# x transposed and weights laid out by chunk on the host, x loaded through buffers of its own

## The chip, the cores and the metric

The kernel runs on one core of a Trainium2 chip. Its time is the device time of one execution in microseconds. A core has five engines with an instruction queue each: PE (TensorE, matrix products), DVE (VectorE), ACT (ScalarE), POOL (GpSimd) and SP (SyncE, which here only issues DMAs), and sixteen DMA engines that they share. Each engine takes its instructions in order.

## What is computed

One layer of a decoder: x is 512 tokens by 2048. One projection gives queries, keys, values and gates for 16 heads of three kinds and six forget gates (`ff`), then attention per head, a gate, an output projection and a layer norm:

```python
h = x @ w_in                                  # 512x2048 @ 2048x8198
(fq, fk, fv, fg, sq, sk, sv, sg, dq, dk, dv, dg, ff) = jnp.split(h, _split_points(), axis=-1)
log_f = jax.nn.log_sigmoid(ff + b_f)
o_fox = forgetting_attention(fq, fk, fv, log_f) * jax.nn.silu(fg)     # 6 heads
o_sb  = stick_breaking_attention(sq, sk, sv) * jax.nn.silu(sg)        # 6 heads
o_d   = differential_attention(dq, dk, dv, lam, slopes)               # 4 heads, rms-normed
o_d   = o_d * subln_g * (1.0 - lam_init) * jax.nn.silu(dg)
y = jnp.concatenate([o_fox, o_sb, o_d], axis=-1) @ w_out
return layernorm(alpha * x + y, ln_g, ln_b)
```

## The kernel before

Every product is made in three passes of a faster, shorter number format (fp32r): an operand is split into a high part (a cast, `h` at the end of its name, on ACT) and a low part (operand minus high part, `l`, on DVE), and `mm3` (line 112) makes high by high, high by low and low by high. So each loaded tile costs a cast and a subtraction before PE can use it (`split`, line 124).

PE contracts over the 128 partitions, so x must lie with its 2048 columns on the partitions: 16 k-tiles of 128 columns by 512 tokens, x0 to x15. x comes as 512 x 2048 from memory. `load_x` (line 303) loads 256 columns at a time, with rows of 1 KB, and `transpose_x` (line 311) turns each k-tile with four PE transposes into a PSUM bank `xt`, from which ACT and DVE take the two parts. For the 12 k-tiles of chunk groups 1 to 3 (`SJ`) ACT also keeps a copy `xc`, from which `x_sums` (line 322) makes four sums on GpSimd (`s`) that are split too (`xs`): they serve a seven-product scheme for the later units (`seven`, line 196).

The first stage multiplies the columns of units 0 and 1 (512 columns) in eight chunks "f" of two k-tiles each (loop at line 725), into four PSUM banks p0a to p0d. Later units u = 2 to 31 have 256 columns and four chunks of four k-tiles ("u", line 161); the attention of the heads runs between them at unit times given by `at_unit`, and `tick` counts those times. At the end come the output projection ("o" chunks) and the layer norm.

Weights are loaded two chunks ahead (`load_chunk`, line 158, on SP) into the tag `raw`, which has three buffers (line 149). The loads of x take buffers of the same tag. A chunk "f" is two DMAs with rows of 1 KB, a chunk "u" one DMA with rows of 1 KB, a chunk "o" one with rows of 2 KB. PE's order is written by hand (`pin`); the order on the other engines is set by a scheduler when the kernel is built.

The start (lines 678 to 699): SP issues the first half of x's first tile, then the weights of the first k-tile, then the other half, then the second k-tile's weights. PE runs five warm-up products, the first transposes, three more warm-ups, and the first product.

Of the kernel before, what the change touches and what calls it, by code (L numbers as in the profile page):

```python
# [70 lines left out]
SEVEN = (1, 5, 7, 6, 2, 4, 3)  # L71
BANK = {1: ("a", 0), 6: ("a", 1), 5: ("b", 0), 7: ("b", 1), 2: ("c", 0), 4: ("c", 1), 3: ("d", 0)}
H2 = S // 2
SECOND = [60] * 7 + [55]


@with_exitstack
def trunk(ctx, tc, x, w_in, b_f, lam_p, subln_g, w_out, ln_g, ln_b, out):
    nc = tc.nc
    V, A, G, T = nc.vector, nc.scalar, nc.gpsimd, nc.tensor  # L80

    xf = x[0]
    w1 = w_in[0].rearrange("(kt p) c -> p kt c", p=P)
    w2 = w_out[0].rearrange("(kt p) c -> p kt c", p=P)
    of = out[0]

    const = ctx.enter_context(tc.tile_pool(name="const", bufs=1))
# [46 lines left out]
    A.preload_act_table_set("natural_log_exp_and_others")  # L134

# [14 lines left out]

        return tuple(wpool.tile(shape, F32R, tag=f"{tag}{s}", bufs=2, name=f"w{s}{name}") for s in "hl")

    def first_cols(k0, k1):
        return [(i * 256, w1[:, k0:k1, c:c + 256]) for i, c in enumerate(head_cols(PAIRS[0][0])[:2])]

    def load_chunk(n):

        kind, g, j = chunks[n]  # L160
        if kind == "u":
            raw = raw_tile(f"raw{n}", [P, 4, 256])
            c0 = head_cols(PAIRS[g // 4][0])[g % 4]
            nc.sync.dma_start(raw, w1[:, 4 * j:4 * j + 4, c0:c0 + 256])
            if j in SJ:
                ready[n] = seven(n, raw)
            else:
                parts = part_tiles(n, [P, 4, 256])
                split(*parts, raw)
                ready[n] = [tuple(t[:, k] for t in parts) for k in range(4)]  # L170
            return
        raw = raw_tile(f"raw{n}", [P, KC, 512])
        if kind == "f":
            for dst, src in first_cols(j * KC, (j + 1) * KC):
                nc.sync.dma_start(raw[:, :, dst:dst + 256], src)
        else:
            k0, c0 = ORDER[j * KC], g * 512
            nc.sync.dma_start(raw, w2[:, k0:k0 + KC, c0:c0 + 512])
        if n >= RES or n % 3 == 2:
            ready[n] = []  # L180
            for k in range(KC):
                if n < RES:
                    hi, lo = part_tiles(f"{n}_{k}", [P, 512], "t2")
                elif slots_left:
                    hi, lo = kx_pair(slots_left.pop(0), [P, 512], f"w{n}_{k}")
                else:
                    hi, lo = [fin.tile([P, 512], F32R, name=f"w{n}_{k}{s}") for s in "hl"]
                ready[n].append((hi, lo))
                pin(A.copy(hi, raw[:, k]))  # L189
                pin(V.tensor_tensor(out=lo, in0=raw[:, k], in1=hi.bitcast(F32), op=ALU.subtract))  # L190
        else:
            parts = part_tiles(n, [P, KC, 512])
            split(*parts, raw)
            ready[n] = [tuple(t[:, k] for t in parts) for k in range(KC)]
# [20 lines left out]
    def load_late(dst, src):  # L215

        pin(nc.sync.dma_start(dst, src))
# [68 lines left out]
    with ExitStack() as actx:  # L286
# [6 lines left out]
            return at.tile([P, 1], F32, tag="st", bufs=24, name=name)  # L293


        xv = xf.rearrange("(tb p) c -> p tb c", p=P)
# [4 lines left out]
        copies = {}  # L301

        def load_x(c):
            xraw[c] = raw_tile(f"xr{c}", [P, NT, 256])
            if c > 0:
                x_part(c, 0, 256)

        def x_part(c, c0, c1):
            nc.sync.dma_start(xraw[c][:, :, c0:c1], xv[:, :, c * 256 + c0:c * 256 + c1])

        def transpose_x(kt):
            c, s = divmod(kt, 2)
            pt = (psL, psL, psT, psO)[kt % 4](f"xt{kt}")
            for tb in range(NT):
                transpose(pt[:, tb * P:(tb + 1) * P], xraw[c][:, tb, s * P:(s + 1) * P], ident)
            for cs, hi, lo in x_parts(kt):
                split(hi, lo, pt[:, cs])
            if kt // 4 in SJ:
                copies[kt] = wk(f"xc{kt}")
                A.copy(copies[kt], pt)  # L320

        def x_sums(j, i):

            ka, kb = copies.pop(4 * j + i), copies.pop(4 * j + 2 + i)
            a11, a21, a12, a22 = ka[:, :H2], ka[:, H2:], kb[:, :H2], kb[:, H2:]
            s = wpool.tile([P, 4, H2], F32, tag="t", bufs=1, name=f"s{j}_{i}")
# [29 lines left out]

        def ff_start():
            wf = at.tile([P, NK, NF], F32, name="wf")
            load_late(wf, w1[:, :, O_FF:O_FF + NF])
            bfc = at.tile([NF, 1], F32, name="bfc")  # L360
            load_late(bfc, b_f.rearrange("a h -> h a"))

# [332 lines left out]
        at_unit(4, lambda: load_x(3))  # L695
        at_unit(7, lambda: load_x(4))
        at_unit(11, lambda: load_x(5))
        at_unit(15, lambda: load_x(6))
        at_unit(19, lambda: load_x(7))
# [15 lines left out]
        acc = [bank(0, b) for b in "abcd"]  # L715

        def product(n, k, c, part=None):
            kt = chunks[n][2] * KC + k
            hi, lo = ready[n][k]
            ps = slice(c * P, (c + 1) * P)  # L720
            for cs, bh, bl in x_parts(kt):
                mm3(acc[c][:, cs], hi[:, ps], lo[:, ps], bh, bl, kt == 0 and cs.start == 0,
                    kt == NK - 1 and cs.stop == S, part)

        for n in range(NJ):
            if n == 0:
                load_chunk(AHEAD)
                for k in range(KC):
                    for part in range(3):
                        for c in range(4):  # L730
                            if k == KC - 1 and part == 2:
                                tick()
                            product(n, k, c, part)
                        if k == 0 and part == 0:
                            transpose_x(1)
                        if k == 1 and part < 2:
                            transpose_x(2 + part)
            for c in range(4) if n > 0 else ():
                if c == 0:
                    load_ahead(n)  # L740
# [204 lines left out]

_INS = ["x", "w_in", "b_f", "diff_lambda", "diff_subln_g", "w_out", "ln_g", "ln_b"]
_OUTS = [((1, S, D), "float32")]


# [20 lines left out]
```

## Time and profile before

| | |
|---|---|
| median of 3 runs | 986.35 us (985.11 to 986.51) |
| the profiled execution | 988.49 us, of which the span shown in the profile is 986.3 |
| PE busy | 962.0 us, 98% of the span |
| DVE busy | 758.6 us, 77% |
| ACT busy | 524.7 us, 53% |
| GpSimd busy | 138.1 us, 14% |
| DMA | 108.76 MB, 110 GB/s in the mean |
| share of the chain that ended last | PE 84%, DVE 6%, DMA 4% |

A row of the order of time reads: start, duration, engine, line, operation, what is written and read, shapes, and in brackets how long the engine had been idle before it and what ended that. Durations of matmuls overlap: the distance from one start to the next is the pace. "PEclk" is the granted clock of PE, where 1.00 is 2.4 GHz and 0.50 is 1.2 GHz. A row of waits reads: who waited for whom, microseconds in total, how often, the longest.

### The profile page before, as it was taken

How to read it: one execution, taken by the hardware profiler on the slowest of the kernel's cores; microseconds unless marked ns; L12 is line 12 of the kernel's file. 1: busy time of each engine (PE TensorE's matmuls, PEld its weight loads, DVE VectorE, ACT ScalarE, POOL GpSimd, SP SyncE). 2: the span in 40 equal slices, each digit the busy share in tenths (PEclk: the TensorE clock that was granted, in tenths of full speed). 3: DMA queues.
4: the chain of work that ended last, by engine and by line, in shares of the span. 5: the costliest groups of instructions: out<-in, count | busy, mean ns of one | idle time of the engine just before them, and what ended most of it. 6: DMA issues, size and time to landing. Idle time of an engine off the chain costs nothing.

```text
span 986.3 us, 16851 instructions
## 1 busy us (share of the span) xinstructions
PE 962.0 (98%) x6466; PEld 882.8 (90%) x6466; DVE 758.6 (77%) x1388; ACT 524.7 (53%) x977; POOL 138.1 (14%) x162
## 2 busy tenths in 40 slices
PE   8998999999999999999999999999999999999994
PEld 7887999999999998999899999999999978888884
DVE  4588888889888988899999887778877863442558
ACT  4665574566466645765675566556745762121222
POOL 0431030113002200120011011010210110000026
PEclk9999999999999999999999999999999999999998
DMA  6443233333332333233323333343333733933313
GB/s 193 150 114 86 67 98 116 86 86 97 97 107 76 108 96 86 73 89 107 98 71 103 106 108 97 99 121 104 105 98 96 224 109 96 348 90 106 98 54 148
DMA packets 92200, 108.76 MB, mean 110 GB/s; under 512 B 6098, under 2 KB 76882, under 8 KB 91864
## 3 DMA queue, kind: packets, MB, share of 16 engines
q1 hardware_dynamic: 88184, 96.15, 33.6%
q10 hardware_dynamic: 3456, 9.96, 2.8%
q0 software_dynamic: 480, 1.57, 0.6%
q8 instruction: 51, 0.84, 0.4%
q14 instruction: 29, 0.24, 0.1%
HBM read 99.80 MB, written 7.88 MB: 109 GB/s over the span
## 4 chain that ended last, share of the span: by engine, by line
PE 84%; DVE 6%; DMA 4%; issue 3%; ACT 2%; SPq 0%; POOL 0%; ACTq 0%; DVEq 0%; POOLq 0%
PE o L107 10%; PE l L107 3%; DMA raw<-in_w_in_dram 3%; PE pt L110 2%; PE po0a L107 1%; PE po0d L107 1%; PE po0c L107 1%; PE po0b L107 1%; PE po2d L107 1%; PE po2c L107 1%; PE po2b L107 1%; PE po2a L107 1%; DVE wl L122 1%; DVE y L906 1%; PE p16c L107 1%
## 5 line engine op out<-in xcount | busy, mean ns | idle before, releaser
L122 DVE TENSOR_TENSOR wlt<-t,wht 128x1024 fp32r<-128x1024 f32 x90 | 110.7, 1230 | 18.0 <-ACT wht L127 17.9
L122 DVE TENSOR_TENSOR wl<-raw,wh 128x1024 fp32r<-128x1024 f32 x53 | 65.3, 1232 | 68.0 <-ACT wh L127 67.6
L127 ACT CAST wht<-t 128x1024 fp32r<-128x1024 f32 x90 | 94.2, 1047 | 28.2 <-DVE t L204 14.7
L127 ACT CAST wh<-raw 128x1024 fp32r<-128x1024 f32 x53 | 55.5, 1048 | 74.9 <-PE po2d L107 27.6
L127 ACT CAST wha<-raw 128x512 fp32r<-128x512 f32 x90 | 55.6, 618 | 48.5 <-PE p18c L107 3.6
L122 DVE TENSOR_TENSOR wla<-raw,wha 128x512 fp32r<-128x512 f32 x90 | 65.7, 730 | 16.8 <-ACT wha L127 16.6
L201 DVE TENSOR_TENSOR t<-raw 128x512 f32<-128x512 f32 x90 | 64.8, 720 | 0.5
L525 ACT ACTIVATE u<-u,m 128x128 f32<-128x128 f32 (+3 forms) x56 | 31.5, 562 | 51.4 <-DVE m L522 51.1
L122 DVE TENSOR_TENSOR wld<-raw,whd 128x256 fp32r<-128x256 f32 x90 | 49.9, 555 | 0.3
L127 ACT CAST pth<-pt 128x128 fp32r<-128x128 f32 (+1 forms) x64 | 26.9, 421 | 23.3 <-PE pt L110 23.2
L204 DVE TENSOR_TENSOR t<-raw,t 128x256 f32<-128x256 f32 x90 | 37.8, 420 | 1.5
L203 DVE TENSOR_TENSOR t<-raw,t 128x256 f32<-128x256 f32 x90 | 38.0, 422 | 0.9
L472 POOL TENSOR_TENSOR g<-g,ge 128x512 f32<-128x512 f32 x16 | 26.9, 1683 | 83.2 <-ACT ge L471 83.2
L127 ACT CAST whd<-raw 128x256 fp32r<-128x256 f32 x90 | 36.0, 400 | 4.5 <-PE p21d L107 1.6
L483 POOL TENSOR_TENSOR mx<-mx,g 128x512 f32<-128x512 f32 x14 | 20.5, 1466 | 119.6 <-issue 101.0
L538 POOL TENSOR_SCALAR_AFFINE_SELECT d<-d 128x128 f32<-128x128 f32 x24 | 14.6, 610 | 160.3 <-ACT d L537 144.8
L122 DVE TENSOR_TENSOR ptl<-pt,pth 128x128 fp32r<-128x128 f32 (+1 forms) x64 | 30.9, 483 | 5.2 <-ACT pth L127 5.0
L901 POOL TENSOR_TENSOR y<-y,gb 128x512 f32<-128x512 f32 (+1 forms) x8 | 12.0, 1521 | 157.8 <-ACT y L900 157.8
L190 DVE TENSOR_TENSOR wl<-raw,wh 128x512 fp32r<-128x512 f32 x22 | 17.0, 792 | 18.7 <-ACT wh L189 18.7
L782 DVE TENSOR_TENSOR e<-e 128x256 f32<-128x256 f32 x30 | 13.7, 456 | 18.9 <-ACT e L781 18.3
L558 POOL TENSOR_SCALAR_AFFINE_SELECT e<-e 128x128 f32<-128x128 f32 x24 | 10.4, 434 | 117.9 <-DVE e L557 98.2
L189 ACT CAST wh<-raw 128x512 fp32r<-128x512 f32 x22 | 13.3, 620 | 25.5 <-PE o L107 11.1
(6721 smaller groups left out, 3849.4 us busy)
## 6 DMA issues: line engine op xcount, KB each, us to landing
raw<-in_w_in_dram SPq DMA_DIRECT2D x120, 512.0 KB, 3.8
raw<-in_w_out_dram SPq DMA_DIRECT2D x32, 512.0 KB, 3.9
xr<-in_x_dram SPq DMA_DIRECT2D x7, 512.0 KB, 3.5
raw<-in_w_in_dram SPq DMA_DIRECT2D x14, 256.0 KB, 4.0
mixd<-mx SPq DMA_DIRECT2D x14, 256.0 KB, 2.0
mr<-mixd ACTq DMA_DIRECT2D x14, 256.0 KB, 4.7
out_dram<-y SPq DMA_DIRECT2D x14, 256.0 KB, 2.4
y<-in_x_dram ACTq DMA_DIRECT2D x4, 768.0 KB, 11.7
```

What stands on the lines that cost most here:

```text
L107: pin(T.matmul(ps, lhs, rhs, start=start, stop=stop))
L110: pin(T.transpose(dst, src, idt))
L122: V.tensor_tensor(out=lo, in0=src, in1=hi.bitcast(F32), op=ALU.subtract)
L127: A.copy(hi, src)
L190: pin(V.tensor_tensor(out=lo, in0=raw[:, k], in1=hi.bitcast(F32), op=ALU.subtract))
L201: V.tensor_tensor(out=t[:, 0:2], in0=raw[:, :, P:].rearrange("p (b k) c -> p b k c", b=2), in1=raw[:, 0:2].rearrange("p k (b c) -> p b k c ...
L203: V.tensor_tensor(out=t[:, 2], in0=b22, in1=t[:, 0], op=ALU.subtract)
L204: V.tensor_tensor(out=t[:, 3], in0=b21, in1=t[:, 2], op=ALU.subtract)
L472: G.tensor_tensor(out=c, in0=c, in1=e, op=ALU.mult)
L483: G.tensor_tensor(out=mx, in0=mx, in1=gt[h], op=ALU.mult)
L525: A.activation(u[:, :n], u[:, :n], AF.Exp, bias=m, scale=-1.0, accum_out=sm)
L538: G.affine_select(out=dt_[:, i * P:n], in_=dt_[:, i * P:n], pattern=[[-1, P]], base=0, channel_multiplier=1, compare_op=ALU.is_ge, fill=BIG)
```

## The change

x is transposed on the host (`x_t`, eight pieces n of two k-tiles, 4 KB for each partition), and the weights are laid out so that each chunk is one run of memory, with 4 KB for each partition. The transposes of x on PE are gone; ACT and DVE split the loaded x itself, and the sums read it too, so the copies `xc` are gone. The pieces of x take the tags `t`, `ptl`, `e` and `pth` (`XTAGS`) in place of `raw`; these tags are used later by the attention and the seven-product scheme. A piece holds k-tiles 4j + i and 4j + i + 2, the pair that a sum needs, and a chunk "f" now multiplies that pair. The first weights are issued by ACT, the first x by SP; the load of ACT's table comes behind them, and the warm-ups stand together: ten.

```diff
+XTAGS = ["t", "ptl", "e", "pth", "ptl", "e", "ptl", "e"]
...
     def load_chunk(n):
...
             raw = raw_tile(f"raw{n}", [P, 4, 256])
-            c0 = head_cols(PAIRS[g // 4][0])[g % 4]
-            nc.sync.dma_start(raw, w1[:, 4 * j:4 * j + 4, c0:c0 + 256])
+            nc.sync.dma_start(raw, w_in[g - 2, j])
...
         if kind == "f":
-            for dst, src in first_cols(j * KC, (j + 1) * KC):
-                nc.sync.dma_start(raw[:, :, dst:dst + 256], src)
+            nc.sync.dma_start(raw, w_first[j])
         else:
-            k0, c0 = ORDER[j * KC], g * 512
-            nc.sync.dma_start(raw, w2[:, k0:k0 + KC, c0:c0 + 512])
+            nc.sync.dma_start(raw, w_out[g, j])
...
-        def load_x(c):
-            xraw[c] = raw_tile(f"xr{c}", [P, NT, 256])
-            if c > 0:
-                x_part(c, 0, 256)
...
-        def transpose_x(kt):
-            c, s = divmod(kt, 2)
-            pt = (psL, psL, psT, psO)[kt % 4](f"xt{kt}")
-            for tb in range(NT):
-                transpose(pt[:, tb * P:(tb + 1) * P], xraw[c][:, tb, s * P:(s + 1) * P], ident)
-            for cs, hi, lo in x_parts(kt):
-                split(hi, lo, pt[:, cs])
-            if kt // 4 in SJ:
-                copies[kt] = wk(f"xc{kt}")
-                A.copy(copies[kt], pt)
-
-        def x_sums(j, i):
-
-            ka, kb = copies.pop(4 * j + i), copies.pop(4 * j + 2 + i)
-            a11, a21, a12, a22 = ka[:, :H2], ka[:, H2:], kb[:, :H2], kb[:, H2:]
+        def load_x(n):
+
+            pool = wpool if XTAGS[n] == "t" else at
+            xraw[n] = pool.tile([P, 2, S], F32, tag=XTAGS[n], bufs=1, name=f"xr{n}")
+            if n > 0:
+                nc.sync.dma_start(xraw[n], xt[n])
+
+        def split_x(n, ks=(0, 1)):
+            j, i = divmod(n, 2)
+            for k in ks:
+                for cs, hi, lo in x_parts(4 * j + 2 * k + i):
+                    split(hi, lo, xraw[n][:, k, cs])
+
+        def x_sums(n):
+
+            j, i = divmod(n, 2)
+            r = xraw.pop(n)
+            a11, a21, a12, a22 = r[:, 0, :H2], r[:, 0, H2:], r[:, 1, :H2], r[:, 1, H2:]
...
         load_x(0)
-        x_part(0, 0, 128)
         first = raw_tile("raw0", [P, KC, 512])
         ready[0] = [part_tiles(f"0_{k}", [P, 512], "t2") for k in range(KC)]
         for k in range(KC):
-            for dst, src in first_cols(k, k + 1):
-                nc.sync.dma_start(first[:, k, dst:dst + 256], src[:, 0])
-            if k == 0:
-                x_part(0, 128, 256)
-                transpose_x(0)
-                warm_up(3)
+            nc.sync.dma_start(xraw[0][:, k], xt[0, :, k])
+            nc.scalar.dma_start(first[:, k], w_first[0, :, k])
+        A.preload_act_table_set("natural_log_exp_and_others")
+        for k in range(KC):
+            split_x(0, (k,))
             hi, lo = ready[0][k]
             V.tensor_copy(hi, first[:, k])
             V.tensor_tensor(out=lo, in0=first[:, k], in1=hi.bitcast(F32), op=ALU.subtract)
+        warm_up(5)
         load_x(1)
         load_chunk(1)
-        at_unit(1, lambda: load_x(2))
...
-        for kt in range(4, NK):
-            at_unit(kt // 2 * 4 - 3 + kt % 2, lambda kt=kt: transpose_x(kt))
-        for n, j in enumerate(SJ):
-            for i in range(2):
-                at_unit(11 + 8 * n + 3 * i, lambda j=j, i=i: x_sums(j, i))
+        load_x(2)
+        split_x(1)
+        for n in range(3, NJ):
+            at_unit(max(1, 4 * n - 11), lambda n=n: load_x(n))
+        for n in range(2, NJ):
+            at_unit(4 * n - 6, lambda n=n: split_x(n))
+        for n in range(NJ):
+            if n // 2 in SJ:
+                at_unit(4 * n + 1, lambda n=n: x_sums(n))
...
         def product(n, k, c, part=None):
-            kt = chunks[n][2] * KC + k
+            kt = n // 2 * 4 + n % 2 + 2 * k
...
-                        if k == 0 and part == 0:
-                            transpose_x(1)
-                        if k == 1 and part < 2:
-                            transpose_x(2 + part)
...
+        x_t=a["x"][0].T.reshape(NK // 4, 2, 2, P, S).transpose(0, 2, 3, 1, 4).reshape(NK // 2, P, 2, S),
+        w_first=_np.concatenate([w1[..., c:c + 256] for c in units[:2]], -1).reshape(
+            NK // 4, 2, 2, P, 512).transpose(0, 2, 3, 1, 4).reshape(NK // 2, P, 2, 512),
+        w_in=_np.stack([w1[..., c:c + 256].transpose(0, 2, 1, 3) for c in units[2:]]),
```

On PE, at the start of the program, the order was (the names: `warm` the warm-ups, `xt` the transposes, `p0a` to `p0d` the four banks of the first stage, `wh` and `wl` the parts of the weights; the number behind a name is that of a buffer):

```order
L107 MATMUL warm<-ones_78 128x128 x5
L110 MATMUL xt_162<-ident,xr_152 128x128 x4
L107 MATMUL warm<-ones_78 128x128 x3
L107 MATMUL p0a<-x0h,wh_0_155 128x512
L107 MATMUL p0b<-x0h,wh_0_155 128x512
L107 MATMUL p0c<-x0h,wh_0_155 128x512
L107 MATMUL p0d<-x0h,wh_0_155 128x512
L110 MATMUL xt_206<-ident,xr_152 128x128 x4
L107 MATMUL p0a<-x0l,wh_0_155 128x512
```

and is now, at the same place:

```order
L106 MATMUL warm<-ones_77 128x128 x10
L106 MATMUL p0a<-x0h,wh_0_153 128x512
L106 MATMUL p0b<-x0h,wh_0_153 128x512
L106 MATMUL p0c<-x0h,wh_0_153 128x512
L106 MATMUL p0d<-x0h,wh_0_153 128x512
L106 MATMUL p0a<-x0l,wh_0_153 128x512
```

The eight warm-ups have become ten in one piece, and products follow on products; no row with `xt` is left on PE, and from the first product of unit 2 on its 5949 rows are those of before.

On SP, from the second load of x in the start on, the order of the DMAs was (`xr` a piece of x, `raw` a chunk of weights):

```order
L309 DMA xr_178<-in_x_dram 128x4x256
L175 DMA raw_180<-in_w_in_dram 128x2x256 x2
L175 DMA raw_191<-in_w_in_dram 128x2x256 x2
L309 DMA xr_244<-in_x_dram 128x4x256
L175 DMA raw_249<-in_w_in_dram 128x2x256 x2
L309 DMA xr_256<-in_x_dram 128x4x256
L309 DMA xr_298<-in_x_dram 128x4x256
L175 DMA raw_306<-in_w_in_dram 128x2x256 x2
```

and is now, from the load of x5 to that of x7 (x5 is `xr_288`, x6 `xr_355`, x7 `xr_418`; `raw_527` and `raw_605` are chunks 8 and 9, the first two of unit 2; `raw_684` is chunk 10):

```order
L298 DMA xr_288<-in_x_t_dram 128x1024
L168 DMA raw_336<-in_w_first_dram 128x1024
L168 DMA raw_403<-in_w_first_dram 128x1024
L168 DMA raw_466<-in_w_first_dram 128x1024
L158 DMA raw_527<-in_w_in_dram 128x1024
L209 DMA wf<-in_w_ff_dram 128x96
L209 DMA bfc<-in_b_f_dram 6x1
L298 DMA xr_355<-in_x_t_dram 128x1024
L158 DMA raw_605<-in_w_in_dram 128x1024
L298 DMA xr_418<-in_x_t_dram 128x1024
L158 DMA raw_684<-in_w_in_dram 128x1024
```

Loads of x and weights took turns before; now the first six pieces of x stand among the first chunks and x6 and x7 stand behind all chunks of the first stage.

## Rows read from the trace of the kernel before

**Rows 1.** Busy time by stage: stretch, length, busy (count) per engine, clock, DMA share, GB/s.
```profile
0.00:64.40 64.40, 60.32 (x344) 52.04 (x345) 37.55 (x68) 36.02 (x72) 17.21 (x27) 0.97 0.59 165
64.40:250.00 185.60, 182.86 (x1342) 171.94 (x1342) 159.98 (x273) 109.53 (x204) 33.13 (x45) 0.99 0.32 90
```

**Rows 2.** Waits of PE, whole run: us in total, times, longest.
```profile
PE pt L110 <- ACT rs L566: 2.7, 1, 2.7
PE l L107 <- DVE vl L122: 2.0, 2, 1.5
PE po0a L107 <- DVE wl L190: 1.2, 1, 1.2
```

**Rows 3.** Chain of waits in the first stage: start, us, what.
```profile
8.57 0.38 SPq L175
...
8.99 3.25 DMA raw<-in_w_in_dram
12.27 1.06 ACT wh L127
...
13.35 1.24 DVE wl L122
14.60 0.37 SPq L175
...
43.38 0.37 SPq L175
```

**Rows 4.** Order of time of PE, start of the run.
```profile
1.12 2.50 PE L107 MATMUL warm<-ones 128*128 128x128 f32 x10 [1.12 <-DVE ones L239]
...
4.59 1.49 PE L107 MATMUL warm<-ones 128*128 128x128 f32 x6
6.00 0.77 PE L107 MATMUL p0a<-x0h,wh 128*128 128x512 f32 x1
...
7.56 0.60 PE L110 MATMUL xt<-ident,xr 128*128 128x128 f32 x4
...
17.72 1.06 PE L110 MATMUL xt<-ident,xr 128*128 128x128 f32 x4
18.43 0.78 PE L107 MATMUL p0b<-x2h,wh 128*128 128x512 f32 x1
```

**Rows 5.** Order of time of PE, later in the first stage.
```profile
21.01 0.60 PE L110 MATMUL xt<-ident,xr 128*128 128x128 f32 x4
21.37 0.48 PE L107 MATMUL p0c<-x2h,wh 128*128 128x512 f32 x1
21.68 0.39 PE L107 MATMUL p0c<-x2l,wh 128*128 128x512 f32 x1
...
57.54 0.28 PE L107 MATMUL p0d<-xa3h,wh 128*128 128x256 f32 x1
...
58.98 0.40 PE L107 MATMUL p0a<-x14h,wh 128*128 128x512 f32 x1
...
64.44 0.28 PE L107 MATMUL p2a<-xa1h,wha 128*128 128x256 f32 x1
```

**Rows 6.** Windows of PE: stretch, length, busy (count), granted clock, DMA share, GB/s.
```profile
18.00:19.00 1.00, 1.00 (x5) 0.50 0.58 156
...
386.00:388.00 2.00, 0.50 (x4) 1.00 0.00 0
...
390.00:392.00 2.00, 2.00 (x11) 0.50 0.64 220
```

**Rows 7.** DMA: GB/s in 40 slices of 0:60, then of 834:860; issues of x, us to landing.
```profile
GB/s 0 193 197 281 282 96 112 285 262 210 222 270 210 178 11 194 374 131 0 134 289 234 41 25 306 129 239 11 1 285 319 94 11 54 307 36 276 60 126 247
...
GB/s 76 236 343 139 28 176 230 199 268 296 290 227 369 432 444 372 372 397 388 369 416 425 425 444 425 444 388 422 457 375 441 419 403 444 400 347 406 378 391 151
...
xr<-in_x_dram SPq DMA_DIRECT2D x7, 512.0 KB, 3.5
```

**Rows 8.** The fourth sum of each set on GpSimd: duration min/median/max in ns.
```profile
L330 POOL TENSOR_TENSOR s<-xc,s x6: 787/858/1072, 32.0 to 73.7; 128x256 f32<-128x256 f32 x6
```

More of the change, by code (lines that the diff above doesn't have):

```diff
@@ L73, with trunk @@
 H2 = S // 2
+XTAGS = ["t", "ptl", "e", "pth", "ptl", "e", "ptl", "e"]
 SECOND = [60] * 7 + [55]
 @with_exitstack
-def trunk(ctx, tc, x, w_in, b_f, lam_p, subln_g, w_out, ln_g, ln_b, out):
+def trunk(ctx, tc, x, xt, w_first, w_in, w_ff, b_f, lam_p, subln_g, w_out, ln_g, ln_b, out):
     nc = tc.nc
@@ L82, in trunk @@
     xf = x[0]
-    w1 = w_in[0].rearrange("(kt p) c -> p kt c", p=P)
-    w2 = w_out[0].rearrange("(kt p) c -> p kt c", p=P)
     of = out[0]
@@ L132, in split @@
                                    op0=ALU.mult, op1=ALU.subtract)
-    A.preload_act_table_set("natural_log_exp_and_others")
     NJ = NK // KC
@@ L153, in part_tiles @@
         return tuple(wpool.tile(shape, F32R, tag=f"{tag}{s}", bufs=2, name=f"w{s}{name}") for s in "hl")
-    def first_cols(k0, k1):
-        return [(i * 256, w1[:, k0:k1, c:c + 256]) for i, c in enumerate(head_cols(PAIRS[0][0])[:2])]
     def load_chunk(n):
@@ L293, in st @@
             return at.tile([P, 1], F32, tag="st", bufs=24, name=name)
-        xv = xf.rearrange("(tb p) c -> p tb c", p=P)
         xraw = {}
@@ L300, in trunk @@
                           for s, (t, b) in zip("hl", ((("g0", 1), ("g1", 1)), (("mx", 2), ("mx", 2)), (("vh0", 1), ("vl0", 1)))[i]))
-        copies = {}
-        def load_x(c):
-            xraw[c] = raw_tile(f"xr{c}", [P, NT, 256])
-            if c > 0:
-                x_part(c, 0, 256)
-        def x_part(c, c0, c1):
-            nc.sync.dma_start(xraw[c][:, :, c0:c1], xv[:, :, c * 256 + c0:c * 256 + c1])
-        def transpose_x(kt):
-            c, s = divmod(kt, 2)
-            pt = (psL, psL, psT, psO)[kt % 4](f"xt{kt}")
-            for tb in range(NT):
-                transpose(pt[:, tb * P:(tb + 1) * P], xraw[c][:, tb, s * P:(s + 1) * P], ident)
-            for cs, hi, lo in x_parts(kt):
-                split(hi, lo, pt[:, cs])
-            if kt // 4 in SJ:
-                copies[kt] = wk(f"xc{kt}")
-                A.copy(copies[kt], pt)
-        def x_sums(j, i):
-            ka, kb = copies.pop(4 * j + i), copies.pop(4 * j + 2 + i)
-            a11, a21, a12, a22 = ka[:, :H2], ka[:, H2:], kb[:, :H2], kb[:, H2:]
-            s = wpool.tile([P, 4, H2], F32, tag="t", bufs=1, name=f"s{j}_{i}")
+        def load_x(n):
[12 more added lines that the diff above has]
+            a11, a21, a12, a22 = r[:, 0, :H2], r[:, 0, H2:], r[:, 1, :H2], r[:, 1, H2:]
+            s = wpool.tile([P, 4, H2], F32, tag="t", bufs=1, name=f"s{n}")
             G.tensor_tensor(out=s[:, 0], in0=a21, in1=a22, op=ALU.add)
@@ L358, in ff_start @@
             wf = at.tile([P, NK, NF], F32, name="wf")
-            load_late(wf, w1[:, :, O_FF:O_FF + NF])
+            load_late(wf, w_ff)
             bfc = at.tile([NF, 1], F32, name="bfc")
@@ L691, in trunk @@
             V.tensor_tensor(out=lo, in0=first[:, k], in1=hi.bitcast(F32), op=ALU.subtract)
+        warm_up(5)
         load_x(1)
         load_chunk(1)
-        at_unit(1, lambda: load_x(2))
[L695 to L699, printed above, removed]
-        for kt in range(4, NK):
-            at_unit(kt // 2 * 4 - 3 + kt % 2, lambda kt=kt: transpose_x(kt))
-        for n, j in enumerate(SJ):
-            for i in range(2):
-                at_unit(11 + 8 * n + 3 * i, lambda j=j, i=i: x_sums(j, i))
+        load_x(2)
[7 more added lines that the diff above has]
+                at_unit(4 * n + 1, lambda n=n: x_sums(n))
         at_unit(40, constants)
@@ L944, in trunk, with _layout @@
         layer_norm(t)
-_INS = ["x", "w_in", "b_f", "diff_lambda", "diff_subln_g", "w_out", "ln_g", "ln_b"]
+_INS = ["x", "x_t", "w_first", "w_in", "w_ff", "b_f", "diff_lambda", "diff_subln_g", "w_out", "ln_g", "ln_b"]
 _OUTS = [((1, S, D), "float32")]
+def _layout(inputs):
+    import numpy as _np
+    a = {k: _np.asarray(v) for k, v in inputs.items()}
+    w1 = a["w_in"][0].reshape(NK // 4, 4, P, -1)
+    units = [head_cols(h)[i] for h, _ in PAIRS for i in range(4)]
+    w2 = a["w_out"][0].reshape(NK, P, D)[ORDER].reshape(NK // KC, KC, P, 4, 512)
+    return dict(
+        a,
+        x_t=a["x"][0].T.reshape(NK // 4, 2, 2, P, S).transpose(0, 2, 3, 1, 4).reshape(NK // 2, P, 2, S),
+        w_first=_np.concatenate([w1[..., c:c + 256] for c in units[:2]], -1).reshape(
+            NK // 4, 2, 2, P, 512).transpose(0, 2, 3, 1, 4).reshape(NK // 2, P, 2, 512),
+        w_in=_np.stack([w1[..., c:c + 256].transpose(0, 2, 1, 3) for c in units[2:]]),
+        w_ff=w1[..., O_FF:O_FF + NF].transpose(2, 0, 1, 3).reshape(P, NK, NF),
+        w_out=w2.transpose(3, 0, 2, 1, 4),
+    )
 def kernel(**inputs):
@@ L959 @@
     nc = _bacc.Bacc("TRN2", target_bir_lowering=False, num_devices=1)
+    inputs = _layout(inputs)
     arrays, args = {}, []
```

## The prediction

> **What bounds the kernel now.** I read the busy time by stage first [rows 1]. PE is busy for 60.32 of the first 64.40 us and for 182.86 of the next 185.60. The first 64.40 us are the stage that the change rewrites: x is loaded, split and multiplied with the first 512 weight columns, in eight chunks of two k-tiles. Its DMA rate is only 165 GB/s and its granted clock 0.97, against 0.99 in the next. Next come PE's waits [rows 2]: three places after the first stage hold 2.7, 2.0 and 1.2 us, the whole run has little more. So PE is the bound nearly everywhere, and time can only be won where PE does work that can go, or where it is slow inside the first stage.
>
> Two things are slow there. The chain of waits [rows 3] shows one closed loop: SP issues a chunk of weights at 8.57, it lands 3.25 us later, ACT takes the high part (1.06), DVE the low part (1.24), and only then, at 14.60, SP issues the next one, since the freed `raw` buffer was what it waited for. x and the weights share three `raw` buffers. From 8.57 to 43.38 the loop turns five times, 6.96 us each. PE's own order of time [rows 4] shows what this does: the first product starts at 6.00, but at 17.72 four transposes that take 0.36 us at 21.01 [rows 5] take 0.71, and the granted clock there is 0.50 [rows 6], that is 1.2 GHz in place of 2.4, after a stretch in which PE had mostly waited for splits.
>
> **Part by part.** The sum is made on the profiled execution: 988.49 us, span 986.3.
>
> *The products themselves* don't change. A 512-wide chunk without transposes goes from 58.98 to 64.44 [rows 5]: 5.46 us for 24 matmuls, 0.2275 each. Twelve 256-wide ones go from 57.54 to 58.98, 0.12 each. Before, five chunks are 512-wide and three are wholly 256-wide: 5 x 5.46 + 3 x 48 x 0.12 = 44.58 us. After, the pairing of k-tiles is another (0 and 2, 1 and 3, and so on), so six chunks are half and half: 2 x 5.46 + 6 x (12 x 0.2275 + 24 x 0.12) = 44.58. Equal.
>
> *The stage before* lasts from 6.00 to 64.44, 58.44 us, so 13.86 us are not products.
>
> *The transposes of x go.* Fifteen groups of four lie inside this stretch. A group and the first product behind it last from 21.01 to 21.68, 0.67 us where a product alone takes 0.2275 [rows 5]: 0.44 each, 15 x 0.44 = 6.6 us. They stand on PE, which has no slack behind them, so this is a plain gain, whether the clock was full or not. The twelve ACT copies that kept x for the sums go too; ACT doesn't set the end, so I cost them at nothing.
>
> *The rest of the 13.86*, 7.26 us, is the slow start of the first four products (6.00 to 7.56, 1.56 us where four take 0.91 [rows 4]: 0.65 us), waits for splits and the half clock. The 0.65 stays, since the same warm-ups stand ahead of it. The other 6.6 us go if the loads come in time.
>
> *Do they?* x now has four tags of its own and `raw` is left to weights, so the loads of chunk 0 to 2 wait for no engine. Before chunk 1 is complete, 2.10 MB must land. In the first microseconds the DMA moved 193, 197, 281 and 282 GB/s in slices of 1.5 us from 1.5 on [rows 7], with runs of 512 B and 1 KB; at their mean, 238, the 2.10 MB are there at 1.5 + 8.8 = 10.3, the high part at 11.4, the low part at 12.6. PE comes to chunk 1 at 6.0 + 0.65 + 5.46 = 12.1 and needs the low part with its third matmul at 12.6. So even the old rate nearly does; where rows of 2 KB and more were moved, the rate was 347 to 457 [rows 7], and by that the data are there at 6 to 8 us. After that one chunk (1.05 MB) needs 4.4 us even at 238 and PE 5.6, so the loads gain on PE. I take 0.4 us of new waits, between 0 and 1.5.
>
> The Trainium skill (DMA: Bandwidth & Descriptors, "Where 436 GB/s comes from") states that for transfers from HBM the HBM side binds at about 358 GB/s for a core. The rows with 444 and 457 lie above it, so here the measurement decides; by 358 chunk 1 would be there at 7.4 and the sum would be the same 973.5.
>
> *The start.* Before, x waited for the transposes and the weights came behind it on SP. After, the ten warm-ups stand in one piece on PE. Each is two records: five took 2.50 us and three took 1.41 from start to start [rows 4], so ten take 4.7 to 5.0 from 1.12 and end at 5.8 to 6.1. The first product needs 512 KB: at 238 GB/s from 1.5 on that is 3.7, and with one cast of x and of w it is ready before 6. So the warm-ups set the start, and it stays at 6.0: the two queues are worth nothing, between -0.3 and +0.3.
>
> The Trainium skill (DMA: Bandwidth & Descriptors, "Rules for kernel authors") speaks against that part as well: DMAs from several issuers run on the same engines, so a second queue saves issue time and brings no bandwidth. The issue time here is 0.43 us for each of the two loads; if it counted, the sum would be 972.6, and by the row on the warm-ups it is 973.5.
>
> *The late x.* `ptl` and `e` each hold several x chunks in turn, so x6 is loaded only when GpSimd has made the four sums of x4, and x7 when it has made those of x5; both stand in SP's queue among the weights of chunks 8 and 9, which wait behind them. A sum takes up to 0.86 us at the median [rows 8], a set 3.4; the next set waits for the splits of the last, which I price like a weight split, 1.06 + 1.24: 5.7 us for a round. x2 lands at 1.5 + 2.62 MB / 238 = 12.5. The sums of x4 end at 12.5 + 2 x 5.7 + 3.4 = 27.3 and x6 lands 3.5 us later [rows 7], 30.8; x7 at 36.5. PE needs them at 40.0 and 45.6. Hidden, with about 7 us to spare after the split.
>
> *What follows the stage.* PE's later rows are the same in the same order, those of ACT, DVE and GpSimd but for a few neighbours. The waits of 2.7, 2.0 and 1.2 us end on splits and weights of units behind this stage [rows 2], made by instructions that stand as before, so I keep them. The weights for later units land sooner, but no wait of PE ends on them: nothing.
>
> Sum: 6.6 + 6.6 - 0.4 = 12.8 us. The profiled execution would be 988.49 - 12.8 = 975.7. It lay 2.14 above the median of the runs, so the median goes from 986.35 to **973.5**.
>
> **Rivals.** (A) *The loop of loads stays the pace.* For it: it fills the chain today. Against: `raw` is now three deep for weights alone. If chunk 7's weights still came at 43.38 + 6.02 (one turn up to the low part), PE would end the stage 5.6 later at 55.0, a gain of 9.4: 977.0. (B) *The DMA rate is the bound.* At the stage's mean of 165 GB/s the 8.39 MB need 50.8 us; with 1.5 ahead and 2.3 + 5.6 behind, the stage ends at 60.2: gain 4.2, 982.1. At 152 GB/s nothing is won. Against: that mean has idle gaps in it, and busy slices were at 281. (C) *Slower: the late x.* A round of sums and splits of r us makes x7 usable at 12.5 + 3r + 3.4 + 3.5 + 2.3; PE stalls from r = 8, and the kernel is slower than before by over 0.2% from r = 13. At r = 14 x7 is 18 us late: 991.6. For it: GpSimd, ACT and DVE run in order, and a split can stand behind a cast that waits for PE. Against: 5.7 from rows. (D) *One new gap and a slow clock.* An idle time of 1.5 us, the longest of the second line [rows 2], lies in the window 386 to 388, and from 390 to 392 the granted clock was 0.50 [rows 6]; the half clock of the first stage lasted from 17.7 to 21.0, which costs half of that, 1.7. Such a gap costs 1.5 + 1.7: 976.7. (E) *The later waits move with the phase:* all three gone, 5.9 less, 967.6, or as much again, 979.4. That the transposes would stay in some form is excluded by PE's order.
>
> **How the numbers follow.** Chances: forecast 0.58 (its own range 972 to 975), A 0.12, B 0.06 (half of it without gain), C 0.04, D 0.08, E 0.06 each way. Beside these the bounds of the new waits are 0 to 1.5. A range from 970 to 979 holds the forecast, A, D and some of E, about 0.8. Faster by over 0.2% (about 2 us, what a measurement here can tell from no change): 0.93; within: 0.03; slower: 0.04.
>
> **What would show it.** Right: no transposes of x; first product near 6.0; PE's first product of unit 2 near 51.5 in place of 64.44; clock 1.00 through that stage; x6 and x7 landing before 40; the wait of 2.7 us still there, some 13 us earlier. Wrong: PE waiting for `wh`, `wl` or x in chunks 1 and 2 (A, B, D), or for x6 and x7 in chunks 6 and 7 (C); a start later than 6.3; PE's time after the stage changed by over 3 us (E).

## The result and the profile after

The changed kernel took 972.84 us at the median of four runs (972.36 to 976.25), the kernel before 986.43 beside it (985.11 to 987.38): a ratio of 0.9871, with a 95% interval of 0.9845 to 0.9896. The forecast was 973.5. The profiled execution of after took 972.67, its span is 970.9; before it was 988.49 and 986.3. So the two profiled executions differ by 15.8 us, the medians by 13.6; the profiled run of before lay 2.1 above its median.

The busy time by stage, in the same columns as [rows 1], with the cut where the first stage now ends:

```profile
0.00:51.40 51.40, 50.27 (x292) 45.11 (x293) 40.62 (x70) 30.75 (x63) 23.22 (x28) 1.00 0.62 206
51.40:237.00 185.60, 182.93 (x1354) 172.05 (x1353) 159.88 (x275) 110.37 (x204) 31.49 (x43) 1.00 0.29 91
```

The first stretch is 13 us shorter than in [rows 1] and PE is busy for all of it but the 1.1 us ahead of the warm-ups; the mean granted clock went from 0.97 to 1.00. The second is as busy as it was (182.93 of 185.60, against 182.86).

PE's order of time at the start and at the end of the stage (start, us, what):

```profile
1.13 4.63 PE L106 MATMUL warm<-ones 128*128 128x128 f32 x20 [1.13 <-DVE ones L231]
5.41 0.68 PE L106 MATMUL p0a<-x0h,wh 128*128 128x512 f32 x1
5.93 0.40 PE L106 MATMUL p0b<-x0h,wh 128*128 128x512 f32 x1
...
50.45 0.28 PE L106 MATMUL p2a<-xa1h,wha 128*128 128x256 f32 x1
```

From the first product to the first of unit 2 it is now 45.04 us, where the products alone are 44.58; in [rows 4, 5] it was 58.44. PE's waits over the whole run (us in total, times, longest):

```profile
PE pt L109 <- ACT rs L551: 2.7, 1, 2.7
PE l L106 <- DVE vl L121: 1.9, 2, 1.5
PE warm L106 <- DVE ones L231: 1.1, 1, 1.1
PE po0a L106 <- DVE wl L182: 0.6, 1, 0.6
```

None lies in the first stage. The three waits of [rows 2] are all still there, some 14 us earlier.

**Where the time went.** Laying PE's rows of both traces side by side and subtracting their starts, the lead of after is 14.0 us at the first product of unit 2 (64.44 against 50.45), and 0.6 of that is the earlier first product. It grows by 1.3 where before ran at 1.2 GHz behind the 2.7 us wait, and by 0.7 in two places behind 780 us (0.6 of it the shorter wait for `po0a`): 15.95 at 928. The tail gives 0.55 back. The 1.3 is the granted clock (last but two in a row) of this stretch of before:

```profile
97.00:98.00 1.00, 1.00 (x7) 1.00 (x6) 1.00 (x3) 0.37 (x1) 0.00 (x0) 0.50 1.02 347
98.00:99.00 1.00, 1.00 (x6) 1.00 (x6) 1.00 (x2) 0.59 (x1) 0.00 (x0) 0.50 0.32 112
```

and of after at the same place of the program:

```profile
83.00:84.00 1.00, 1.00 (x11) 1.00 (x10) 1.00 (x2) 0.90 (x2) 0.00 (x0) 1.00 0.89 365
```

The wait ahead of it was 2.7 us in both kernels, and the clock fell in one of the two executions. It isn't the change that decides this, as the run with one queue shows below.

### The profile page after: what moved, and what is told of

It reads as the page before. It is cut to its first block, busy times and chain, and to the rows that moved or that the text cites. A ratio compares the mean times of both kernels' runs of the same rounds, so it can differ in the third digit from the quotient of the medians.

```text
span 970.9 us, 16701 instructions
## 1 busy us (share of the span) xinstructions
PE 949.8 (98%) x6406; PEld 873.8 (90%) x6406; DVE 759.1 (78%) x1388; ACT 518.7 (53%) x965; POOL 141.9 (15%) x162
## 4 chain that ended last, share of the span: by engine, by line
PE 89%; DVE 5%; issue 3%; DMA 1%; ACT 1%; POOL 0%; ACTq 0%; SPq 0%; DVEq 0%; POOLq 0%
PE o L106 10%; PE l L106 3%; PE pt L109 2%; PE p0a L106 1%; PE p0b L106 1%; PE po0a L106 1%; PE po0b L106 1%; PE po0d L106 1%; PE po0c L106 1%; PE po2d L106 1%; PE po2c L106 1%; PE po2b L106 1%; PE po2a L106 1%; PE p0c L106 1%; PE p0d L106 1%
## 5 line engine op out<-in xcount | busy, mean ns | idle before, releaser
L106 PE MATMUL o<-ptl,vh 128*128 128x256 f32 x96 | 26.9, 280 | 0.0
```

The lines of the kernel that those rows point to most:

```text
L106: pin(T.matmul(ps, lhs, rhs, start=start, stop=stop))
```

## The experiments

### What the transposes of x cost by themselves

The changed kernel, with 15 groups of four PE transposes of a constant put where the transposes of x had stood; nothing reads them.

```diff
+        def idle_transposes(kt):
+            pt = (psL, psL, psT, psO)[kt % 4](f"xt{kt}")
+            for tb in range(NT):
+                transpose(pt[:, tb * P:(tb + 1) * P], ident, ident)
...
+        for kt in range(4, NK):
+            at_unit(kt // 2 * 4 - 3 + kt % 2, lambda kt=kt: idle_transposes(kt))
...
+                        if k == 0 and part == 0:
+                            idle_transposes(1)
+                        if k == 1 and part < 2:
+                            idle_transposes(2 + part)
```

> The changed kernel with 15 groups of four PE transposes (of the identity, read by nobody) put back at the places where those of x stood; loads, buffers and splits stay as changed. Theory (PE is the bound in the first stage, so each group costs 0.44 us there): 15 x 0.44 = 6.6 us slower than the changed kernel, about 979.5 us, the stage ending near 57.0 in place of 50.45, no wait of PE in it. Rival (the transposes lay in time in which PE would have waited for loads, and the loads are the gain): within 1 us of 972.8.

Measured: 979.23 us (978.75 to 982.22), ratio 0.9936 [0.9915, 0.9957], so 6.4 more than after. Its first product starts at 5.20, and the stage ends here:

```profile
56.74 0.28 PE L106 MATMUL p2a<-xa1h,wha 128*128 128x256 f32 x1
```

That is 51.54 us, 6.5 more than after, or 0.43 for a group; the prediction read 0.44 from [rows 5]. No wait came with them. The transposes are a plain cost on the engine that sets the end, and they are half of the gain.

### The other half: own buffers, the layout, and both

Three runs look for the other half. First before's kernel with x in the four tags of its own and nothing else changed:

```diff
-            xraw[c] = raw_tile(f"xr{c}", [P, NT, 256])
+            pool = wpool if XTAGS[c] == "t" else at
+            xraw[c] = pool.tile([P, NT, 256], F32, tag=XTAGS[c], bufs=1, name=f"xr{c}")
```

> The kernel before with one edit: the pieces of x take the tags t, ptl, e and pth in place of raw; transposes, short rows and the order of the first loads stay. Theory: the waits and the half clock of the first stage go, 5 to 6.6 us faster than before, 980 to 981.5 us; the 15 groups of transposes stay. Rival (short rows at 250 to 280 GB/s keep the pace): within 2 us of 986.4.

Measured: 983.53 (981.54 to 984.57), ratio 0.9971 [0.9958, 0.9983]: 3.0 us less than before, so between the two expectations. There is no half clock in its stage (granted 1.00 throughout, in this one execution), yet the stage still takes 54.96 us from 6.01:

```profile
60.97 0.28 PE L108 MATMUL p2a<-xa1h,wha 128*128 128x256 f32 x1
```

Second, before's kernel with only the weights laid out by chunk:

```diff
-            for dst, src in first_cols(j * KC, (j + 1) * KC):
-                nc.sync.dma_start(raw[:, :, dst:dst + 256], src)
+            nc.sync.dma_start(raw, w_first[j])
```

> The kernel before with one edit: all weights laid out by chunk, so that each chunk is one run of memory with 4 KB for each partition; x, its transposes and the three raw buffers stay. Theory: a load in the loop of the first stage lands some 1 us sooner, 1 to 3 us faster than before in all, 983 to 985.5 us, since the loop itself stays; nothing in the later units, where no wait of PE ends on a load. Rival (the layout carries the gain): 6 us faster or more, 980 us.

Measured: 986.23 (982.81 to 988.96), ratio 0.9999 [0.9985, 1.0014]: nothing, where 1 to 3 us had been expected. The loads of the loop in its chain of waits (start, us, what):

```profile
8.63 3.57 DMA raw<-in_w_first_dram
22.07 4.28 DMA raw<-in_w_first_dram
28.78 4.67 DMA raw<-in_w_first_dram
36.63 4.29 DMA raw<-in_w_first_dram
43.35 4.44 DMA raw<-in_w_first_dram
```

SP issues the chunks at the times at which it issued them before ([rows 3] has 8.57 and 43.38). A load in longer rows isn't shorter here ([rows 3] has 3.25 us for the first). That fits a loop that is set by when a `raw` buffer comes free.

Third, both edits together on before's kernel.

> The kernel before with both edits that were tried alone: the pieces of x in tags of their own, and the weights laid out by chunk; x's short rows, its transposes on PE and the order of the first loads stay. Theory 1 (the two need each other: own buffers put more loads in flight, and only then the rate of the loads counts): more than the sum of 3.0 and 0.3 us, 5 to 6.5 us faster than before, 980 to 981.5 us, the stage ending near 58. Theory 2 (what is left after own buffers is the detour of x through PE: load, transposes, split, product): as with own buffers alone, 983 to 984 us.

Measured: 982.43 (979.5 to 985.41), ratio 0.9953 [0.9936, 0.9969]: 4.6 less than before, between the two expectations. Their single gains add up to 3.3 (3.0 and 0.3 by medians), and the intervals of this run and the first meet, so whether the two edits help each other isn't settled. A table of the stage, worked out from the starts of the first product and of unit 2's first in each profile:

| kernel | first product | end of stage | length |
|---|---|---|---|
| before | 6.00 | 64.44 | 58.44 |
| before, own buffers | 6.01 | 60.97 | 54.96 |
| before, own buffers and layout | 5.63 | 59.90 | 54.27 |
| after, idle transposes | 5.20 | 56.74 | 51.54 |
| after | 5.41 | 50.45 | 45.04 |

The third and fourth line do the same work on PE, but in the third x goes from its load through PE's transposes into PSUM, and only then to the splits. Of the 2.7 us between them 2.1 are waits of PE for x (the row below, and 0.3 for `xb3l`). The order of the first loads and the rows of x differ there too, so the detour alone isn't shown to be the cause.

```profile
PE p0a L106 <- DVE x0l L121: 1.8, 1, 1.8
```

### Own buffers taken back

The other way round: after's kernel with x in the three `raw` buffers again.

```diff
-            pool = wpool if XTAGS[n] == "t" else at
-            xraw[n] = pool.tile([P, 2, S], F32, tag=XTAGS[n], bufs=1, name=f"xr{n}")
+            xraw[n] = raw_tile(f"xr{n}", [P, 2, S])
```

> The changed kernel with x loaded through the three raw buffers that the weights use, as before the change; no transposes, long rows. Theory (the buffers of its own are what ended the loop of loads): the loop comes back, the stage ends near 55 to 58 and the time is 977 to 980 us, with PE waiting for wh, wl or x splits in the first chunks and a half clock there. Rival (the long rows, read at 402 to 419 GB/s, are what ended it, three buffers would do): within 1 us of 972.8.

Measured: 985.07 (981.99 to 987.07), ratio 0.9986 [0.9969, 1.0002], 12.2 more than after: nearly the whole gain is lost, more than was expected. SP issues the weights of the first stage about 6.5 us apart again, from 9.63 to 42.16, nearly the 6.96 of [rows 3], and unit 2 begins 8.4 us later than in after:

```profile
58.87 0.39 PE L106 MATMUL p2a<-xa1h,wha 128*128 128x256 f32 x1 [3.65 <-DVE ql L130]
```

The stage's own products end at 55.2, in the range that was expected; 3.65 of the 8.4 are the wait in this row, for a split on DVE that stands there behind the split of late weights. What the expectations had missed: a piece of x is now read by its sums too, so it holds its `raw` buffer until GpSimd has made them, and SP, which waits for that buffer, has the next loads behind it. Four of SP's issues follow the fourth sum of a set within 0.03 us, as here (first GpSimd, then SP):

```profile
15.78 1.06 POOL L314 TENSOR_TENSOR s<-xr,s 128x256 f32<-128x256 f32 x1
...
16.87 0.33 SPq L168 DMA_DIRECT2D raw<-in_w_first_dram  x1
```

The wait `pt` also grew from 2.7 to 3.9 us, and behind the wait of 3.65 and behind `pt` the granted clock fell to 0.50 here, which cost PE 1.6 and 1.4 us against its rows in after. So in the changed kernel the gain from the transposes hangs on the buffers being apart.

### Two queues

The first weights back on SP, and ACT's table first:

```diff
+    A.preload_act_table_set("natural_log_exp_and_others")
...
-            nc.scalar.dma_start(first[:, k], w_first[0, :, k])
-        A.preload_act_table_set("natural_log_exp_and_others")
+            nc.sync.dma_start(first[:, k], w_first[0, :, k])
```

> The changed kernel with the first two weight loads issued by SP between the first two loads of x, and the table load of ACT ahead of everything, as before. Theory (the warm-ups set the start): the first product stays at 5.4 and the time within 1 us of 972.8. Rival (two queues bring the data sooner): first product 0.5 to 1 us later.

Measured: 974.26 (971.27 to 975.21), ratio 0.987 [0.9848, 0.9893], not to be told from after by time. The first product starts at 5.42, against 5.41. Yet unit 2 begins at 51.45 in this profile, 1.0 later than in after, and PE waits 0.3 us for the low part of chunk 1's weights. So the second queue, or the place of ACT's table load that moved with it, may be worth up to 1 us; one execution of each doesn't show it.

Behind its `pt` wait this execution fell to 1.2 GHz, where after's did not:

```profile
86.00:88.00 2.00, 2.00 (x11) 2.00 (x11) 1.93 (x5) 0.52 (x1) 0.29 (x1) 0.50 0.00 0
```

The wait of 1.5 us for `vl` shows the opposite. It ends at 374.92 here and at 372.65 in after; behind it this execution stayed at full clock, and after's (the second row) did not:

```profile
376.00:378.00 2.00, 2.00 (x18) 2.00 (x18) 1.94 (x6) 1.93 (x4) 0.00 (x0) 1.00 0.83 231
...
376.00:378.00 2.00, 2.00 (x12) 2.00 (x12) 1.92 (x4) 0.00 (x0) 0.00 (x0) 0.52 0.03 12
```

So a slow stretch behind one and the same wait comes and goes between executions, at 1 to 2 us each. That fits the 3 to 4 us by which runs of one kernel differ here; that it is all of it isn't shown.

### Rows of 1 KB

After's kernel, with the weights read from the old layout.

```diff
-            nc.sync.dma_start(raw, w_first[j])
+            k0 = j // 2 * 4 + j % 2
+            for i, c in enumerate(head_cols(PAIRS[0][0])[:2]):
+                nc.sync.dma_start(raw[:, :, i * 256:i * 256 + 256], w1[:, k0:k0 + 3:2, c:c + 256])
```

> The changed kernel with the weights in their old layout: rows of 1 KB, two loads for each of the first chunks; x stays transposed with rows of 4 KB and in tags of its own. Theory 1 (the rate counts once buffers are free): the first product and chunks 1 and 2 wait 1 to 3 us for weights, 974 to 976 us. Theory 2 (buffers and the missing detour are all): within 1 us of 972.8.

Measured: 974.02 (971.91 to 975.8), ratio 0.9873 [0.9845, 0.99]. It can't be told from after by time; the profile has the first product 0.7 later and the stage's end 0.9 later:

```profile
6.10 0.47 PE L108 MATMUL p0a<-x0h,wh 128*128 128x512 f32 x1 [0.90 <-DVE wh L680]
```

So by this profile the layout is worth about 1 us, all at the start, and nothing once loads run ahead of PE. The time is just inside the range of theory 1, but none of its waits came in chunks 1 and 2.

### The start: five warm-ups fewer

After's kernel without `warm_up(5)`.

```diff
-        warm_up(5)
```

> The changed kernel with five warm-ups in place of ten. They end near 3.3, the first splits are ready at 5.1. Theory: the first product moves from 5.41 to 5.1 and the time by 0.3 us at most. Rival (the idle time of 1.8 us between warm-ups and products is followed by a half clock as after the idle times of 1.5 and 2.7 us elsewhere): 1.7 us more in the first chunk, about 974.5 us.

Measured: 974.58 (974.04 to 974.85), ratio 0.9877 [0.9862, 0.9892], 1.7 more than after, as the rival said. PE's order of time:

```profile
5.26 0.76 PE L106 MATMUL p0a<-x0h,wh 128*128 128x512 f32 x1 [1.63 <-DVE wh L673]
...
6.25 0.63 PE L106 MATMUL p0c<-x0h,wh 128*128 128x512 f32 x1
...
10.94 0.56 PE L106 MATMUL p0b<-x2h,wh 128*128 128x512 f32 x1
11.34 0.40 PE L106 MATMUL p0c<-x2h,wh 128*128 128x512 f32 x1
11.57 0.40 PE L106 MATMUL p0d<-x2h,wh 128*128 128x512 f32 x1
```

The operands were ready at 5.26, only 0.15 ahead of after's start, so the warm-ups delay almost nothing. Without the five, products follow one another by 0.43 us up to 11 us and by 0.23 from 11.34 on: half speed for 6 us, and the stage ends 2.4 us later, at 52.85. Yet the column for the granted clock (the third from the end) says 1.00 there:

```profile
7.00:8.00 1.00, 1.00 (x4) 0.71 (x4) 1.00 (x3) 0.84 (x2) 0.00 (x0) 1.00 1.00 410
```

At 0.43 us a product that microsecond holds 2.3 of them, at the later pace it would hold 4.3. In before products followed one another by the same 0.43 us where the column read 0.50 (18 to 19 us, [rows 6]):

```profile
19.01 0.63 PE L107 MATMUL p0b<-x2l,wh 128*128 128x512 f32 x1
19.43 0.63 PE L107 MATMUL p0b<-x2h,wl 128*128 128x512 f32 x1
```

So by the pace PE was at 1.2 GHz here, and the column can't be right. Whether the clock had never risen since the program began or had fallen in the idle time of 1.63 us, as the rival has it, the record doesn't show. The Trainium skill (TensorE: Matmul & The Clock Gate, "What's actually happening") states that the slow clock is the default and that activity lifts it; the pace of this run agrees with it, the record of the clock doesn't. By that reading the record misses the state in which the program starts, and the slow first products of before (0.65 us in the prediction) were the last at 1.2 GHz; in that kernel I have not tried it.

### The late x: how much slack there is

After's kernel, with the first sum of each set made five times on GpSimd.

```diff
-            G.tensor_tensor(out=s[:, 0], in0=a21, in1=a22, op=ALU.add)
+            for _ in range(5):
+                G.tensor_tensor(out=s[:, 0], in0=a21, in1=a22, op=ALU.add)
```

> The changed kernel with the first sum of each set on GpSimd made five times over (the same result): 3 to 5 us more for each set before the buffer of that piece of x comes free. Theory (a round of sums and splits takes 7.4 us as measured, x7 is usable some 2 us before PE needs it, so a round of 11 us makes it late): PE waits in chunks 6 and 7 for x6 and x7 and in unit 2 for the sums, 8 to 16 us slower than the changed kernel, 981 to 989 us. Rival (the late pieces have much to spare): within 2 us of 972.8.

Measured: 984.35 (981.81 to 985.76), ratio 0.9965 [0.994, 0.9989], 11.5 more than after, as expected. SP's issues of x6 and x7, and the waits that they made on PE:

```profile
41.03 0.33 SPq L298 DMA_DIRECT2D xr<-in_x_t_dram  x1
...
50.51 0.33 SPq L298 DMA_DIRECT2D xr<-in_x_t_dram  x1
...
PE p0a L106 <- ACT xa3h L126: 6.4, 2, 5.7
```

In after x6 was issued at 31.37 and x7 at 36.62; here they come 9.7 and 13.9 us later. PE waits 5.7 us for x6 and 0.7 for x7, the granted clock is 0.50 from 44 to 49 us behind the first of these waits, and the stage ends 10.3 later, at 60.72. A round that is only a few us longer stalls PE: the mechanism of rival C is real.

### Taking the 2.7 us wait away

Two runs go after the wait `pt`, which the change left alone: PE comes to a transpose of attention weights before ACT has made their last exponential. For the first head of the first pair the transposes are put one unit, then two units later (`lag` goes from 8 to 9 and to 10), and the products with v that follow them keep their place.

```diff
-            attend(ha, 64 * p + 34, every, lag, 5)
+            attend(ha, 64 * p + 34, every, lag + (p == 0), 5 - (p == 0))
```

> The changed kernel with the transposes of the first head's weights (pt, 2.7 us of PE waiting for ACT rs) placed one unit of PE's work later for the first pair of heads, and what follows them left where it was. Theory (the wait is a fault of the place, since PE has other products to do): the wait and the half clock that can follow it go, 2.7 to 4 us faster than the changed kernel, 969 to 970.5 us. Rival (PE then waits elsewhere, in the products with v that follow sooner behind the transposes): within 1 us of 972.8.

```diff
-            attend(ha, 64 * p + 34, every, lag, 5)
+            attend(ha, 64 * p + 34, every, lag + 2 * (p == 0), 5 - 2 * (p == 0))
```

> The same with two units. Theory: as with one unit, 969 to 970.5 us, if one unit is enough; if one unit left part of the wait, lower than that one by the part. Rival: the splits of the transposes come too late for the products with v, which follow three units behind: 1 to 3 us slower than with one unit.

Measured: 971.27 (969.03 to 972.75), ratio 0.9844 [0.9817, 0.987], and 970.05 (968.84 to 972.0), ratio 0.9839 [0.981, 0.9869]. PE's waits of the second:

```profile
PE l L106 <- DVE vl L121: 1.9, 2, 1.5
...
PE vp L109 <- DVE rs L548: 0.8, 1, 0.8
PE po0a L106 <- DVE wl L182: 0.3, 1, 0.3
```

The 2.7 us wait is gone in both and one of 0.8 has come, at a later use of `rs`. The first kernel lands 0.8 us above the range that was expected, the second inside it. By medians the second kernel is 2.8 us below after, and its four runs lie below after's four; the intervals against before overlap, so the size of this step is not measured. It is the fastest kernel of this study, and faster than before beyond doubt.

## Why the prediction held, point by point

**The transposes:** 6.6 forecast, 6.4 measured by time, 6.5 by the stage. The step held because it asked first whether the engine is the bound and then took the cost from a neighbour with and without a group [rows 5].

**Waits and half clock:** 6.6 forecast. Of the 14.0 us at the stage's end 0.6 are the start and 6.5 the transposes, so 6.9 are left. The mechanism held in part. In the profile with own buffers alone the loop is broken (SP has issued all weights of the stage by 25 us, where the last came at 43.38 [rows 3]) and the half clock is gone; with the layout alone it is there, as in before (0.50 at 18 to 20 us). But own buffers give only 3.0 us; the rest of this term came only in the kernels that split x as loaded. The prediction gave all of it to loads that come in time and didn't price the way of x through PE and PSUM by itself; how much of the rest that was isn't shown.

**New waits in chunk 1:** 0.4 forecast, none came. x and weights landed faster than the 238 GB/s by which the forecast reckoned. After's DMA, GB/s in 40 slices of 0:52:

```profile
GB/s 0 85 337 402 418 416 419 419 406 407 406 340 239 217 309 91 302 41 0 180 224 0 76 310 93 211 161 126 296 176 217 9 85 318 60 328 16 0 0 0
```

The bracket's upper end (347 and more, from [rows 7]) was the right one. But row length, to which the prediction put the difference, isn't the main reason. With weights in rows of 1 KB (after's kernel) the slices from 2.6 to 13 us had 301 to 423. And before's kernel with own buffers alone, its rows as short as before, had these GB/s in 40 slices of 0:60:

```profile
GB/s 0 198 204 298 229 343 289 318 382 355 349 350 344 327 296 238 57 307 23 0 0 0 134 343 248 18 25 236 371 73 5 60 289 0 0 0 0 88 262 0
```

From 5 to 20 us that is 285 to 346 in each 5 us, where before had 175 to 253, and before's kernel with only the weights laid out by chunk 142 to 268. So what held the rate down was mainly that SP could issue few loads before a buffer came free. Longer rows add to it once it can: from 5 to 15 us after had 408 to 415, and with weights in rows of 1 KB 329 to 363.

**The start:** 6.0 +/- 0.3 forecast, 5.41 measured, outside the bound. The step that failed took ten warm-ups as 4.7 to 5.0 us from [rows 4], where groups stood apart. In one piece ten start within 4.28 us. That warm-ups and not loads set the start held narrowly: the first operands were ready at 5.08, 0.3 ahead, and in the run with transposes a unit later, whose start is after's, PE waited 0.5 for `x0h`. That two queues are worth nothing held by time; by the profile of one run they may be worth up to 1 us. That the ramp of 0.65 stays did not quite: the first product takes 0.52 to the next, and then they are at full pace, 0.3 in all.

**The late x:** about 7 us to spare forecast; 1.6 measured for x7 in the same terms, and 1.1 for x6. x7's last low part is ready at 43.25 and chunk 7 begins at 44.83; x6's is ready at 38.15 and chunk 6 begins at 39.20. (The products that read these parts start at 45.77 and 40.14, so 2.5 and 2.0 us were really left.) This is the step that was furthest off, and only slack hid it. The rows for x6, of DVE and of PE:

```profile
37.47 0.68 DVE L121 TENSOR_TENSOR x14l<-xr,x14h 128x512 fp32r<-128x512 f32 x1
...
39.20 0.28 PE L106 MATMUL p0a<-xa3h,wh 128*128 128x256 f32 x1
```

The sets of four sums end on GpSimd at 14.36, 24.40, 31.34 and 36.60: rounds of 10.0, 6.9 and 5.3 us, in the mean 7.4, where the prediction had 5.7 and put the first stall at 8. Of the 7.4 the sums took 4.9, where 3.4 were forecast, and the wait for the split ahead of them 2.5, where 2.3 were: so the price of a set of sums is the term that was wrong. The two engines beside each other (start, us, what), GpSimd:

```profile
9.96 1.49 POOL L312 TENSOR_TENSOR s<-xr 128x256 f32<-128x256 f32 x1 [3.98 <-DMA xr<-in_x_t_dram]
...
18.21 2.93 POOL L312 TENSOR_TENSOR s<-xr 128x256 f32<-128x256 f32 x1 [3.85 <-DVE xs_3l L121]
21.10 0.73 POOL L313 TENSOR_TENSOR s<-xr 128x256 f32<-128x256 f32 x1
```

and DVE:

```profile
10.78 0.96 DVE L121 TENSOR_TENSOR xa1l<-xr,xa1h 128x256 fp32r<-128x256 f32 x1
...
18.05 1.21 DVE L121 TENSOR_TENSOR wl<-raw,wh 128x1024 fp32r<-128x1024 f32 x1
19.19 0.41 DVE L121 TENSOR_TENSOR xa2l<-xr,xa2h 128x256 fp32r<-128x256 f32 x1
19.52 0.41 DVE L121 TENSOR_TENSOR xb2l<-xr,xb2h 128x256 fp32r<-128x256 f32 x1
19.86 0.68 DVE L121 TENSOR_TENSOR x10l<-xr,x10h 128x512 fp32r<-128x512 f32 x1
```

The add that starts at 18.21 takes 2.93 us, the next of its kind 0.73. DVE has four subtractions end to end from 18.05 to 20.54, and the add ends 0.60 later, at 21.14: it looks as if it ran only when DVE stopped. With five subtractions end to end, in the run with rows of 1 KB, the same add takes 4.06 and ends 0.59 behind the last of them (GpSimd, then DVE's fifth):

```profile
19.19 4.06 POOL L318 TENSOR_TENSOR s<-xr 128x256 f32<-128x256 f32 x1 [4.45 <-DVE xs_3l L123]
...
21.44 1.22 DVE L123 TENSOR_TENSOR wl<-raw,wh 128x1024 fp32r<-128x1024 f32 x1
```

In after at 10.78 it is the other way round, with subtractions of 0.96 in place of 0.41 while GpSimd adds. The Trainium skill (SBUF — State Buffer, "SBUF: two separate sides") states just this: a DVE operation with two SBUF inputs and a GpSimd operation that reads SBUF take one pair of ports by turns, each for a whole instruction. The rows agree, with 2.93 against 0.73. Before shows it too, beside a subtraction on weights:

```profile
49.46 1.73 POOL L329 TENSOR_TENSOR s<-s,xc 128x256 f32<-128x256 f32 x1
...
48.85 1.74 DVE L122 TENSOR_TENSOR wl<-raw,wh 128x1024 fp32r<-128x1024 f32 x1 [0.87 <-ACT wh L127]
50.51 0.41 DVE L122 TENSOR_TENSOR xa3l<-xt,xa3h 128x256 fp32r<-128x256 f32 x1
```

The add ends 0.60 behind `wl`, and the split of `xt`, which lies in PSUM, runs beside it and doesn't hold it up. The change turned these splits into ones that read `xr` in SBUF, and so made the collision more frequent; the prediction priced both engines from rows of before. No run was made to take the one engine away; the cause is read from the traces, where the add's length follows DVE's subtractions on SBUF operands.

**What follows:** waits kept, forecast right; the 1.3 us gained behind `pt` was chance of one execution, and lies inside the 2.1 by which before's profiled run was above its median.

**The rivals.** A and B fell with the stage's end at 50.45 (A wanted 55.0, B 60.2). C didn't decide, by the little that was left for x6 and x7. D had no gap to start from. E: the later waits stayed; what differed behind the stage was mainly the clock behind one of them, 1.3 us.

## What to carry to other kernels

A buffer that is shared between two streams couples them: ask of each tile who reads it last, since the last reader sets when the other stream's next load is issued. Taking work off the bound engine is worth its full time only if nothing else is as late: here the transposes gone without buffers of x's own gave 1.4 us (not clear of noise), the buffers alone 3.0, and the whole change 13.6. And a stretch at an odd pace is found by the distance of like instructions, not by the clock column alone, above all at the start of a program.

## What the runs showed of the hardware that was not expected

- At the start PE ran matmuls of 512 columns 0.43 us apart in place of 0.23 for 6 us, while the record of the granted clock read 1.00.
- A GpSimd add of 128x256 took 2.93 us in place of 0.73 beside four subtractions of DVE on SBUF operands and 4.06 beside five, and such subtractions took 0.96 in place of 0.41 beside GpSimd.
- Behind one and the same wait (2.7 us in before and after) TensorE's clock fell to 0.50 in one execution and stayed at 1.00 in another.
